# A residual-add and RMSNorm kernel: every bulk transfer cut into two halves of 64 partitions

## Chip, cores and metric

The kernel runs on one core of one Trainium2 chip. The metric is the device time of one execution in microseconds (us); lower is better. The record marks each run as fast or slow, by its clock and its time against its fellows. Repeated runs of the kernel before agree within 0.03%.

## The reference

```python
# x, residual: (32, 2048, 2048) float32; gamma: 2048 ones; eps 1e-6
z = x + residual
rms = np.sqrt(np.mean(z ** 2, axis=-1, keepdims=True) + eps)
return (z / rms * gamma).astype(np.float32)
```

65536 rows of 8 KB: two inputs are read, one output is written, 1610.6 MB in all.

## The kernel before

Rows lie on the 128 partitions of SBUF, the on-chip memory, R = 7 consecutive rows on each partition. The first two tiles have 3 and 5 rows per partition, the other 72 have 7. For each tile one transfer loads x into one of two buffers `z`, one loads the residual into a shared area; VectorE adds in place, ScalarE squares and sums, VectorE scales in place, and one transfer stores `z`. One queue (SP) issues all of it. A transfer raises its semaphore by U = 16 (the trace has 3712 landings for 232 transfers, 16 each).

```python
    def rows(t, i):
        k = sizes[i]
        return t[starts[i] : starts[i] + P * k, :].rearrange("(p r) m -> p r m", r=k)
    # ... (cut)
    def load_x(sp, t, d=0):
        i = t.i + d
        inc(sp.dma_start(out=z[i % 2][:, : sizes[i], :], in_=rows(x_f, i)), "x_in", i)
    # ... load_r likewise (cut)
    def sp_turn(sp, t):
        i = t.i
        t.wait(sp, "done", -1)         # tile i-1 is scaled
        inc(sp.dma_start(out=rows(o_f, i - 1), in_=z[(i - 1) % 2][:, : sizes[i - 1], :]), "s_out", i - 1)
        if i == last:
            return
        t.wait(sp, "add_a")            # first part of tile i is added
        load_r(sp, t, 1)
        t.wait(sp, "s_out", -1)        # tile i-1 is stored, its z is free
        # ... the last tile's x comes in four pieces (cut)
        load_x(sp, t, 1)
```

Of the kernel before, what the change touches and what calls it, by code (L numbers as in the profile page):

```python
# [9 lines left out]
def kernel(  # L10
# [18 lines left out]
    P = nc.NUM_PARTITIONS  # L29
# [4 lines left out]
    x_f = x.flatten_outer_dims()  # L34
    r_f = residual.flatten_outer_dims()
    o_f = out.flatten_outer_dims()
# [1 line left out]
    n_rows, D = x_f.shape  # L38
    R = 7
    STEP = 4  # L40
    U = 16
    lead = [3, 5]
    n_full = (n_rows // P - sum(lead)) // R
    sizes = lead + [R] * n_full
# [5 lines left out]
    last = n_tiles - 1  # L50
# [6 lines left out]
# [3 lines that stand above are left out]
# [3 lines left out]
    def sb(name, shape):  # L63
        return ctx.enter_context(nc.sbuf_tensor(name, shape, fp32))
# [6 lines left out]
    def sem(name):  # L71
        sems.append(ctx.enter_context(nc.semaphore(name)))
        return sems[-1]
# [3 lines left out]
    z = [sb(f"z{p}", [P, R, D]) for p in range(2)]  # L77
    r_area = sb("r_area", [P, R + STEP, D])
# [12 lines left out]
    ev = {k: [sem(f"{k}{p}") for p in range(2)] for k in names}  # L91
    x_tail = [sem(f"x_tail{k}") for k in range(4)]
    g_in = sem("g_in")
    dve = sem("dve_own")
    act = sem("act_own")
    s_tail = sem("s_tail")
# [6 lines left out]
    def entry(i):  # L103
        if i == 0:
            return R + STEP - sizes[0]
        return 0 if i % 2 else STEP
# [7 lines left out]
    class Turn:  # L114
# [5 lines left out]
        def at(self, d):  # L120

            n = ((self.i + d) // 2 + 1) * U
            return n if self.it is None else self.it * (U // 2) + n

# [3 lines left out]
    def inc(ins, kind, i):  # L128
        return ins.then_inc(ev[kind][i % 2], U)


    def load_x(sp, t, d=0):
        i = t.i + d
        inc(sp.dma_start(out=z[i % 2][:, : sizes[i], :], in_=rows(x_f, i)), "x_in", i)

    def load_r(sp, t, d=0):
        i = t.i + d
        e = entry(i)
        inc(
            sp.dma_start(out=r_area[:, e : e + sizes[i], :], in_=rows(r_f, i)),  # L140
            "r_in",
            i,
        )

    def sp_turn(sp, t):
        i = t.i
        t.wait(sp, "done", -1)
        inc(
            sp.dma_start(out=rows(o_f, i - 1), in_=z[(i - 1) % 2][:, : sizes[i - 1], :]),
            "s_out",  # L150
            i - 1,
        )
        if i == last:
            return
        t.wait(sp, "add_a")
        load_r(sp, t, 1)
        t.wait(sp, "s_out", -1)
        if i + 1 == last:
            for k, (a, b) in enumerate(tail):
                sp.dma_start(  # L160
                    out=z[last % 2][:, a:b, :], in_=rows(x_f, last)[:, a:b, :]
                ).then_inc(x_tail[k], U)
        else:
            load_x(sp, t, 1)


    def add(v, i, a, b):
        e = entry(i)
        s = z[i % 2][:, a:b, :]
        return v.tensor_add(out=s, in0=s, in1=r_area[:, e + a : e + b, :])  # L170

    def scale(v, i, a, b, rs, c=0):
        for g in range(a, b):
            s = z[i % 2][:, g, :]
            ins = v.scalar_tensor_tensor(  # L175
                out=s,
                in0=s,
                scalar=rs[:, c + g - a : c + g - a + 1],
                in1=gamma_tile[:, :],
                op0=mult,  # L180
                op1=mult,
            )
        return ins

    def dve_turn(v, t, own):
        i, p = t.i, t.p
        t.wait(v, "x_in")
        t.wait(v, "r_in")
        (a0, b0), (a1, b1) = parts(i)
        inc(add(v, i, a0, b0), "add_a", i)  # L190
        inc(add(v, i, a1, b1), "add_b", i)
        for h, (a, b) in enumerate(parts(i)):
            n = b - a
            t.wait(v, "rms_a" if h == 0 else "rms_b")
            v.reciprocal(out=rstd[p][h][:, :n], in_=rms[p][h][:, :n]).then_inc(dve, U)  # L195
            v.wait_ge(dve, own(i, h))
            ins = scale(v, i, a, b, rstd[p][h])
        inc(ins, "done", i)
# [50 lines left out]
    def sync_program(sp):  # L249
        load_x(sp, Turn(0))  # L250
        load_r(sp, Turn(0))

        sp.wait_ge(tail_ev["add"], 1)
        for q in range(4):
            sp.dma_start(  # L255
                out=stage[32 * q : 32 * q + 1],
                in_=gamma.partition_broadcast(1).rearrange("p (a b) -> p a b", a=16),
            ).then_inc(g_in, U)
        load_r(sp, Turn(1))
        load_x(sp, Turn(1))  # L260
        for i in range(1, n_tiles):
            sp_turn(sp, Turn(i))
        for k, (a, b) in enumerate(tail):
            sp.wait_ge(tail_ev["done"], k + 1)
            sp.dma_start(
                out=rows(o_f, last)[:, a:b, :], in_=z[last % 2][:, a:b, :]
            ).then_inc(s_tail, U)
        sp.wait_ge(s_tail, U * len(tail))
        sp.wait_ge(ev["s_out"][(last - 1) % 2], ((last - 1) // 2 + 1) * U)
        sp.sem_inc(fin, 1)  # L270

    def vector_program(v):
        v.memset(eps_tile[:, :], float(eps))  # L273
        v.memset(stage, 0.0).then_inc(tail_ev["add"], 1)  # L274
        v.wait_ge(g_in, 4 * U)
        v.stream_shuffle(gamma_tile[:, :].rearrange("p (a b) -> p a b", a=16), stage, [0] * 32)  # L276
        for i in range(LO):
            dve_turn(v, Turn(i), lambda i, h: (2 * i + h + 1) * U)
        with v.Fori(0, 2 * n_iter, 2) as it:
            for i in range(LO, LO + 2):  # L280
                dve_turn(v, Turn(i, it), lambda i, h: it * (2 * U) + (2 * i + h + 1) * U)
        for i in range(HI, last):
            dve_turn(v, Turn(i), lambda i, h: (2 * i + h + 1) * U)
        base = 2 * last * U
        t = Turn(last)
        t.wait(v, "r_in")

        def tail_scale(k):
            a, b = tail[k]
            v.wait_ge(tail_ev["rms"], k + 1)  # L290
            v.reciprocal(out=tail_rstd[:, a:b], in_=tail_rms[:, a:b]).then_inc(dve, U)  # L291
            v.wait_ge(dve, base + (k + 1) * U)
            scale(v, last, a, b, tail_rstd, a).then_inc(tail_ev["done"], 1)

        for k, (a, b) in enumerate(tail):
            v.wait_ge(x_tail[k], U)
            add(v, last, a, b).then_inc(tail_ev["add"], 1)
            if k:
                tail_scale(k - 1)
        tail_scale(len(tail) - 1)  # L300

    def scalar_program(s):
# [13 lines left out]
        for k, (a, b) in enumerate(tail):  # L316
# [4 lines left out]
            ).then_inc(tail_ev["rms"], 1)  # L321

    sync_program(nc.sync)
    vector_program(nc.vector)
    scalar_program(nc.scalar)

# [40 lines left out]
```

## Time and profile before

| | kernel before |
|---|---|
| time, median | 3726.5 us |
| transfers: busy share, rate | 99.9%, 434 GB/s in the steady part |
| VectorE / ScalarE busy | 62% / 29% |
| bulk transfers | 228 |
| tile period | 50.8 us |
| packet of 57344 B (one partition of a full tile) | 2.116 us |

The page, the stretch from 1000 to 2000 us, the queue's issues and two links of the chain are shown and read in the prediction: the transfer engines run without a gap (99.9%) at a fixed pace (99.7% of the packets of 57344 B took below 2.22 us), and all else hides behind them. The packet row needs a remark. Besides the page, the trace records each packet's size, start and duration, and each transfer's landings, but no engine number. I take a landing, and the small packet that goes with it (3712 of each in the kernel before), as one for each engine that took part.

### The profile page before, as it was taken

How to read it: one execution, taken by the hardware profiler on the slowest of the kernel's cores; microseconds unless marked ns; L12 is line 12 of the kernel's file. 1: busy time of each engine (PE TensorE's matmuls, PEld its weight loads, DVE VectorE, ACT ScalarE, POOL GpSimd, SP SyncE). 2: the span in 40 equal slices, each digit the busy share in tenths (PEclk: the TensorE clock that was granted, in tenths of full speed). 3: DMA queues.
4: the chain of work that ended last, by engine and by line, in shares of the span. 5: the costliest groups of instructions: out<-in, count | busy, mean ns of one | idle time of the engine just before them, and what ended most of it. 6: DMA issues, size and time to landing. Idle time of an engine off the chain costs nothing.

```text
span 3724.7 us, 3652 instructions
## 1 busy us (share of the span) xinstructions
DVE 2302.5 (62%) x816; ACT 1072.4 (29%) x1176; POOL 0.2 (0%) x4
## 2 busy tenths in 40 slices
DVE  5666665566665566665566665566665566655566
ACT  2233322233322233322233322233322233322233
POOL 0000000000000000000000000000000000000000
DMA  9999999999999999999999999999999999999999
GB/s 420 432 434 434 434 434 434 432 434 434 435 434 434 434 434 436 434 434 434 433 434 434 434 434 434 434 434 434 434 434 434 434 434 434 434 434 434 434 434 398
DMA packets 32964, 1610.69 MB, mean 432 GB/s; under 512 B 3712, under 2 KB 3776, under 8 KB 3776
## 3 DMA queue, kind: packets, MB, share of 16 engines
q1 hardware_dynamic: 32960, 1610.66, 99.9%
q14 instruction: 4, 0.03, 0.0%
HBM read 1073.77 MB, written 536.87 MB: 432 GB/s over the span
## 4 chain that ended last, share of the span: by engine, by line
DMA 66%; DVE 22%; issue 9%; ACT 2%; SPq 0%; DVEq 0%; ACTq 0%
DMA out_dram<-z 33%; DMA z<-in_x_dram 33%; DVE z L170 15%; DVE z L175 7%; ACT sq_junk L221 1%; DMA r_area<-in_gamma_dram 0%; ACT rms L229 0%; DVE rstd L195 0%; DVEq L126 0%; SPq L255 0%; DVE r_area L274 0%; ACTq L209 0%; ACTq L126 0%; DVE tail_rstd L291 0%; SPq L160 0%
## 5 line engine op out<-in xcount | busy, mean ns | idle before, releaser
L170 DVE TENSOR_TENSOR z<-z,r_area 128x8192 f32<-128x8192 f32 (+2 forms) x150 | 1109.4, 7437 | 1253.2 <-DMA z<-in_x_dram 1227.6
L221 ACT ACTIVATE sq_junk<-z 128x2048 f32<-128x2048 f32 x512 | 963.4, 1882 | 2618.1 <-DVE z L170 2606.7
L175 DVE SCALAR_TENSOR_TENSOR z<-z,rstd,gamma_tile 128x2048 f32<-128x2048 f32 x505 | 1153.5, 2344 | 5.2
L195 DVE RECIPROCAL rstd<-rms 128x4 f32<-128x4 f32 (+2 forms) x146 | 25.3, 173 | 130.8 <-ACT rms L229 130.8
L221 ACT ACTIVATION_READ_ACCUMULATOR sq_junk<-z 128x1 f32 x512 | 95.4, 186 | 0.0
L229 ACT ACTIVATE rms<-ssq,eps_tile 128x4 f32<-128x4 f32 (+2 forms) x146 | 43.3, 297 | 13.4
L175 DVE SCALAR_TENSOR_TENSOR z<-z,tail_rstd,gamma_tile 128x2048 f32<-128x2048 f32 x7 | 16.2, 2346 | 0.1
L276 DVE LOAD_MASK_SELECT gamma_tile<-r_area x1 | 0.0, 14 | 16.4 <-DMA r_area<-in_gamma_dram 16.4
L276 DVE STREAM_SHUFFLE gamma_tile<-r_area 128x2048 f32<-128x2048 f32 x1 | 2.3, 2290 | 0.0
L274 DVE MEMSET r_area<- 128x2048 f32 x1 | 1.8, 1765 | 0.4 <-issue 0.4
L221 ACT ACT_TABLE_LOAD x1 | 1.3, 1283 | 0.9 <-SPq L75 0.9
L229 ACT ACT_TABLE_LOAD x1 | 1.3, 1283 | 0.1
L229 ACT ACTIVATE tail_rms<-tail_ssq,eps_tile 128x2 f32<-128x2 f32 (+1 forms) x4 | 1.2, 296 | 0.1
L273 DVE MEMSET eps_tile<- 128x1 f32 x1 | 0.1, 59 | 1.0 <-SPq L75 1.0
L291 DVE RECIPROCAL tail_rstd<-tail_rms 128x2 f32<-128x2 f32 (+1 forms) x4 | 0.6, 158 | 0.0
L348 POOL MEMSET const-bfloat16-1.0<- 128x1 bf16 x1 | 0.1, 102 | 0.0
L348 POOL MEMSET const-uint8-127<- 128x1 uint8 x1 | 0.1, 102 | 0.0
L348 POOL MEMSET const-float32-1.0<- 128x1 f32 x1 | 0.1, 99 | 0.0
L348 POOL MEMSET const-float32-0.0<- 128x1 f32 x1 | 0.1, 98 | 0.2 <-issue 0.2
## 6 DMA issues: line engine op xcount, KB each, us to landing
r_area<-in_residual_dram SPq DMA_DIRECT2D x72, 7168.0 KB, 27.2
z<-in_x_dram SPq DMA_DIRECT2D x71, 7168.0 KB, 33.8
out_dram<-z SPq DMA_DIRECT2D x71, 7168.0 KB, 34.5
z<-in_x_dram SPq DMA_DIRECT2D x3, 2048.0 KB, 26.3
out_dram<-z SPq DMA_DIRECT2D x3, 2048.0 KB, 13.9
r_area<-in_residual_dram SPq DMA_DIRECT2D x1, 5120.0 KB, 25.3
z<-in_x_dram SPq DMA_DIRECT2D x1, 5120.0 KB, 36.8
out_dram<-z SPq DMA_DIRECT2D x1, 5120.0 KB, 24.7
```

What stands on the lines that cost most here:

```text
L170: return v.tensor_add(out=s, in0=s, in1=r_area[:, e + a : e + b, :])
L175: ins = v.scalar_tensor_tensor(out=s, in0=s, scalar=rs[:, c + g - a : c + g - a + 1], in1=gamma_tile[:, :], op0=mult, op1=mult,)
L195: v.reciprocal(out=rstd[p][h][:, :n], in_=rms[p][h][:, :n]).then_inc(dve, U)
L221: s.activation(out=sq_junk[:, :], in_=src[:, g, :], func=Act.Square, accum_out=sq[:, g - a : g - a + 1],)
L229: return s.activation(out=rm, in_=sq[:, : b - a], func=Act.Sqrt, bias=eps_tile[:, :], scale=inv_d)
L273: v.memset(eps_tile[:, :], float(eps))
L274: v.memset(stage, 0.0).then_inc(tail_ev["add"], 1)
L276: v.stream_shuffle(gamma_tile[:, :].rearrange("p (a b) -> p a b", a=16), stage, [0] * 32)
L291: v.reciprocal(out=tail_rstd[:, a:b], in_=tail_rms[:, a:b]).then_inc(dve, U)
L348: nc = _bacc.Bacc("TRN2", target_bir_lowering=False, num_devices=1)
```

## The change

The intent: each of the 16 transfer engines should have 4 packets in each of two transfers, instead of 8 in one (a transfer before has 128 packets of data, one for each partition, and 16 landings). The core of the diff (the call sites are cut; all bulk loads and stores go through `move`):

```diff
-    U = 16
+    U = 32
+    def move(sp, out, in_, s):
+        for h in range(2):
+            c = slice(h * P // 2, (h + 1) * P // 2)
+            sp.dma_start(out=out[c], in_=in_[c]).then_inc(s, 16)
@@ load_x, and so on
-        inc(sp.dma_start(out=z[i % 2][:, : sizes[i], :], in_=rows(x_f, i)), "x_in", i)
+        move(sp, z[i % 2][:, : sizes[i], :], rows(x_f, i), ev["x_in"][i % 2])
```

Below, A is the lower half (partitions 0 to 63) and B the upper (64 to 127).

More of the change, by code (lines that the diff above doesn't have):

```diff
@@ L138, in load_r @@
         e = entry(i)
-        inc(
-            sp.dma_start(out=r_area[:, e : e + sizes[i], :], in_=rows(r_f, i)),
-            "r_in",
-            i,
-        )
+        move(sp, r_area[:, e : e + sizes[i], :], rows(r_f, i), ev["r_in"][i % 2])
     def sp_turn(sp, t):
@@ L147, in sp_turn @@
         t.wait(sp, "done", -1)
-        inc(
-            sp.dma_start(out=rows(o_f, i - 1), in_=z[(i - 1) % 2][:, : sizes[i - 1], :]),
-            "s_out",
-            i - 1,
-        )
+        move(sp, rows(o_f, i - 1), z[(i - 1) % 2][:, : sizes[i - 1], :], ev["s_out"][(i - 1) % 2])
         if i == last:
@@ L159, in sp_turn @@
             for k, (a, b) in enumerate(tail):
-                sp.dma_start(
-                    out=z[last % 2][:, a:b, :], in_=rows(x_f, last)[:, a:b, :]
-                ).then_inc(x_tail[k], U)
+                move(sp, z[last % 2][:, a:b, :], rows(x_f, last)[:, a:b, :], x_tail[k])
         else:
@@ L257, in sync_program @@
                 in_=gamma.partition_broadcast(1).rearrange("p (a b) -> p a b", a=16),
-            ).then_inc(g_in, U)
+            ).then_inc(g_in, 16)
         load_r(sp, Turn(1))
@@ L264, in sync_program @@
             sp.wait_ge(tail_ev["done"], k + 1)
-            sp.dma_start(
-                out=rows(o_f, last)[:, a:b, :], in_=z[last % 2][:, a:b, :]
-            ).then_inc(s_tail, U)
+            move(sp, rows(o_f, last)[:, a:b, :], z[last % 2][:, a:b, :], s_tail)
         sp.wait_ge(s_tail, U * len(tail))
@@ L274, in vector_program @@
         v.memset(stage, 0.0).then_inc(tail_ev["add"], 1)
-        v.wait_ge(g_in, 4 * U)
+        v.wait_ge(g_in, 4 * 16)
         v.stream_shuffle(gamma_tile[:, :].rearrange("p (a b) -> p a b", a=16), stage, [0] * 32)
```

## The prediction

The forecast's sum came to 7271 + 10 us: 7271 is 3709.6 us at the full rate times 1.96. No trace of the kernel before shows that factor, 2 less 0.04 for a lead of 0.3 us between engines. The 217 GB/s is half of the 434 measured. "In step" means that all 16 engines are on the same half at a time.

> **What bounds the kernel now.** I read the page's overview first: which engine is busy, and how busy the transfers are.
>
> ```profile
> DVE 2302.5 (62%) x816; ACT 1072.4 (29%) x1176; POOL 0.2 (0%) x4
> DMA  9999999999999999999999999999999999999999
> DMA packets 32964, 1610.69 MB, mean 432 GB/s; under 512 B 3712, under 2 KB 3776, under 8 KB 3776
> q1 hardware_dynamic: 32960, 1610.66, 99.9%
> HBM read 1073.77 MB, written 536.87 MB: 432 GB/s over the span
> ```
>
> No compute engine is above 62%, the transfer engines are at nine tenths or more in all forty slices, and their packets fill 99.9% of the span of 16 engines. Next I asked for a long stretch far from both ends.
>
> ```profile
> 1000.00:2000.00 1000.00, 624.21 (x220) 292.27 (x320) 0.00 (x0) 1.00 1.00 434
> ```
>
> The columns are the stretch, its length, the busy time of DVE, ACT and POOL, the clock, the transfer share (1.00) and GB/s (434). So the kernel streams at one rate: 1610.69 MB at 434.2 GB/s (16 engines at 27.1) take 3709.6 us, and only 15 of the 3724.7 us are left for start and end. The trace also has each packet's duration: a packet of 57344 bytes (7 rows of 2048 float32, one partition of a full tile) takes 2.116 us at the median, 27.1 GB/s for its engine, with almost no scatter. The engines run at a fixed pace.
>
> Then the issuing queue, in time order near the end of the steady part, and two links of the chain of waits there:
>
> ```profile
> 3594.36 0.33 SPq L140 DMA_DIRECT2D r_area<-in_residual_dram  x1
> 3604.67 0.33 SPq L134 DMA_DIRECT2D z<-in_x_dram  x1
> 3620.98 0.34 SPq L149 DMA_DIRECT2D out_dram<-z  x1
> 3645.16 0.33 SPq L140 DMA_DIRECT2D r_area<-in_residual_dram  x1
> ...
> 3553.85 33.84 DMA z<-in_x_dram
> 3620.98 34.47 DMA out_dram<-z
> ```
>
> One tile period is 3645.16 - 3594.36 = 50.8 us, three transfers of 7.34 MB at 434 GB/s (16.9 us each). The x load lands 33.84 us after its issue: 16.9 behind the residual load already queued, 16.9 of its own. The store takes 34.47 for the same reason. The tightest point is the residual load, issued 10.3 us (3604.67 - 3594.36) before the engines have finished the store in front of it. The queue never runs dry, so neither waits nor issue cost count; only the rate does.
>
> [...] no transfer here covers 64, so the half rate is not shown. [...] 228 bulk transfers and 4 of gamma, times 16 completions, are the 3712 packets under 512 B. [...]
>
> **The change part by part.**
> *Bytes and data packets*: unchanged. 74 residual loads, 77 x loads (four are the pieces of the last tile) and 77 stores become 456 transfers of 64 partitions, with one packet for each partition as before; 228 x 16 = 3648 completion packets are added, of 9 ns each in this trace: 2 us per engine, little.
> *Issue*: 228 more issues of 0.34 us, 78 us of a queue that otherwise waits (1689.2 us for the add, 1190.8 for the scale). Per tile 1.0 us, and each second half is queued long before the first is through: beside the work.
> *Waits*: the unit of every transfer semaphore rises from 16 to 32, so each wait is still for a whole tile; VectorE's and ScalarE's order and shapes are the same. Nothing to pay or gain.
> [...]
> *Relief from drift*: [...] From the trace's landing records (16 for each transfer) I took the spread between the first and the last engine: about 1.1 us in the first 200 us, 3.3 at 900, 6.6 at the end, where one engine trails. [...]
> *Ends*: at half rate the last x pieces and the last stores are always queued behind transfers, so idle time there shrinks; I leave 10 us for start and the last landing.
> Sum: 7271 + 10[...]: I say 7270.
>
> **The rivals.**
> 1. *Engines slip out of step*: [...] Then the full 434 GB/s return: 3727 to 3760 us. [...] I give 0.11.
> 2. *Only loads are limited*: [...] Then 1073.77 MB at 217 (4946 us) and 536.87 at 434 (1236): 6182 us. [...] About 0.1.
> 3. *Partial overlap*: [...] Some 0.15 together.
> 4. *A gain*: an earlier half lets nothing start earlier, as all waits are for both halves[...]. Only the 15 us at the ends could shrink: 0.4%. Faster by 2% would need a rate of 443: 0.01.
>
> **Range and chances.** In step (7100 to 7450) I hold at 0.63; with rivals 2 and 3 the range from 6150 to 7480 holds a little over 8 in 10. Slower by over 2%: 0.88; within 2%: 0.11; faster: 0.01.
>
> **What would show it.** In the profile of the changed kernel: (a) slices at 217 to 222 GB/s instead of 434, with the transfer share still at nine tenths or above, because the packets take longer, not because the queue is dry. (b) Packets of 57344 bytes near 4.2 us instead of 2.116; 2.1 for those of stores would be rival 2; 2.1 for all is rival 1. (c) A tile period near 101 us (6 x 16.9) instead of 50.8. (d) VectorE's and ScalarE's busy times as before; VectorE's share falls to 31 or 32%, its wait for x grows from 1227.6 to about 4900 us. (e) Residual loads landing about 44 (A) and 61 us (B) after issue instead of 27.2: the 10.3 of the store's remainder become 27, plus 16.9 for each half. (f) 7360 small packets, (456 + 4) x 16; fewer would mean that a half does not run on 16 engines and that my engine picture is wrong. The prediction fails if the rate stays near 434 with (f) as said[...].

## The result, and the profile after

The changed kernel takes 7100.4 us (median of 4, 7042.9 to 7108.3), 1.9025 times the time before (95% interval 1.8938 to 1.9112). Ratios here are the mean time of one kernel's fast runs over that of the other's of the same rounds, so not quite the ratio of the medians quoted. The prediction of 7270 us (6150 to 7480) was 2.4% above. The profiled execution is the fastest one, of 7041.1 us.

The page of the changed kernel, the lines that answer to those shown of before:

```profile
DVE 2302.6 (33%) x816; ACT 1072.4 (15%) x1176; POOL 0.2 (0%) x4
DMA  9999999999999999999999999999999999999999
DMA packets 36614, 1610.72 MB, mean 229 GB/s; under 512 B 7360, under 2 KB 7424, under 8 KB 7424
q1 hardware_dynamic: 36608, 1610.67, 99.7%
```

The busy times and the bytes are the same, the engines are as busy as before (99.7%, 99.9% then), and the rate is about half (229 GB/s, 432 then). The busy share cannot tell the two kernels apart; the rate and the packets' durations can (4.005 us at the mean for one of 57344 B, 2.118 before).

The same stretch as before, the queue's issues, and one link of the chain of the changed kernel, each from its own view (the columns are those of the same views of before):

```profile
1000.00:2000.00 1000.00, 314.12 (x110) 146.12 (x160) 0.00 (x0) 1.00 1.00 227
```
```profile
3076.79 3.21 SPq L135 DMA_DIRECT2D r_area<-in_residual_dram  x2
3098.16 1.28 SPq L135 DMA_DIRECT2D z<-in_x_dram  x2
3103.41 1.13 SPq L135 DMA_DIRECT2D out_dram<-z  x2
3173.74 3.22 SPq L135 DMA_DIRECT2D r_area<-in_residual_dram  x2
```
```profile
3103.39 63.69 another core or an unknown queue
```

The tile period is 3173.74 - 3076.79 = 97.0 us instead of 50.8. The store is now issued 5.3 us after the x load, before even the residual load is through, which lands 56.6 us after its first issue at the median (before the change the store came 16.3 us after the x load): VectorE is done long before, and the transfers alone set the pace. The chain's "another core or an unknown queue" is the wait for x. Why the chain does not name it is not known (in `e1_rows` below two transfers raise one semaphore as well, and there it is named). The waits of the compute engines do name it, and how long it was:

```profile
DVE z L165 <- DMA z<-in_x_dram: 4537.5, 74, 65.6
```

VectorE waits 4537.5 us for x in all, 1227.6 before.

Of the packets of 57344 B, from the trace's packet records:

| kernel | mean us | median us | below 2.22 us | 2.22 to 4 us | above 4 us |
|---|---|---|---|---|---|
| before | 2.118 | 2.116 | 99.7% | 0.3% | 0 |
| after | 4.005 | 4.384 | 7% | 18% | 75% |

The mean accounts for the time: 3709.6 x 4.005 / 2.118 = 7015 us, of the 7041 in this execution.

### The profile page after: what moved, and what is told of

Read it like the earlier page. It is cut to its first block, busy times and chain, and to the rows that moved or that the text cites. A ratio compares the mean times of both kernels' runs of the same rounds, so it can differ in the third digit from the quotient of the medians.

```text
span 7041.1 us, 3880 instructions
## 1 busy us (share of the span) xinstructions
DVE 2302.6 (33%) x816; ACT 1072.4 (15%) x1176; POOL 0.2 (0%) x4
## 2 busy tenths in 40 slices
DMA packets 36614, 1610.72 MB, mean 229 GB/s; under 512 B 7360, under 2 KB 7424, under 8 KB 7424
## 3 DMA queue, kind: packets, MB, share of 16 engines
q1 hardware_dynamic: 36608, 1610.67, 99.7%
## 4 chain that ended last, share of the span: by engine, by line
another core or an unknown queue 64%; DVE 23%; issue 9%; ACT 2%; DMA 1%; DVEq 0%; SPq 0%; ACTq 0%
DVE z L165 16%; DVE z L170 7%; ACT sq_junk L216 1%; DMA z<-in_x_dram 1%; DMA r_area<-in_gamma_dram 0%; ACT rms L224 0%; DVE rstd L190 0%; SPq L135 0%; DVEq L126 0%; DVEq L272 0%; SPq L250 0%; ACTq L204 0%; ACTq L126 0%; DVE tail_rstd L284 0%
## 5 line engine op out<-in xcount | busy, mean ns | idle before, releaser
L165 DVE TENSOR_TENSOR z<-z,r_area 128x8192 f32<-128x8192 f32 (+2 forms) x150 | 1109.4, 7437 | 4537.5 <-DMA z<-in_x_dram 4537.5
```

The costliest lines, as they stand in the source:

```text
L165: return v.tensor_add(out=s, in0=s, in1=r_area[:, e + a : e + b, :])
```

## The experiments

Twelve kernels ran, for five questions. All give the right result except two that say so. Kernels that were run together ran on one chip, and the kernel before ran beside each of them.

**Is it the number of transfers?** `e1_rows` has as many transfers, issues and completions as the change, but cuts each by rows.

```diff
-            c = slice(h * P // 2, (h + 1) * P // 2)
-            sp.dma_start(out=out[c], in_=in_[c]).then_inc(s, 16)
+            # cut = (k + 1) // 2 of the k rows; a single row is cut by columns
+            c = (slice(None), slice(0, cut) if h == 0 else slice(cut, k))
+            sp.dma_start(out=out[c], in_=in_[c]).then_inc(s, 16)
```

> Every bulk transfer in two as in the change, but cut by rows: 456 transfers of all 128 partitions. [...] packets run at 27.1 GB/s as in the kernel before, and the time is 3727 us, at most 3740. Rival, that 456 transfers instead of 228, their issues, completions or waits for two cost the time: about 7100 us as in the changed kernel, or at least well above 4000.

Measured: 3741.5 us, ratio 1.0041 (1.0024 to 1.0058). The number of transfers costs 15 us, not 3374. The packets alone account for that: those of 4 and 3 rows took 1.2146 and 0.9141 us at the mean, together 10.5 ns more than one of 7 rows, which is 18 us over the 1712 that each engine moves. The page of this run has as many small packets (7360, the completions) as that of the changed kernel:

```profile
DMA packets 65798, 1610.72 MB, mean 431 GB/s; under 512 B 7360, under 2 KB 7424, under 8 KB 7936
```

**Loads or stores?** `e2_loads` halves the loads by partitions and cuts the stores by rows; `e3_stores` is the mirror.

```diff
# e2_loads: the stores
-        move(sp, rows(o_f, i - 1), z[(i - 1) % 2][:, : sizes[i - 1], :], ...)
+        rows_move(sp, rows(o_f, i - 1), z[(i - 1) % 2][:, : sizes[i - 1], :], ...)
# e3_stores: the loads
-        move(sp, z[i % 2][:, : sizes[i], :], rows(x_f, i), ...)
+        rows_move(sp, z[i % 2][:, : sizes[i], :], rows(x_f, i), ...)
```

The sums of 5940 and 4820 us below are for both directions slowed, each by a factor of 1.9.

> Loads in halves of 64 partitions as in the change, stores cut by rows (128 partitions). [...] the loads are two thirds of the bytes, so 3710 x (2/3 x 1.9 + 1/3) = about 5940 us; packets of loads near 4.4 us, of stores 2.1. Only loads limited (rival): about as slow as the whole change, 7000 to 7100 us. Only stores limited: 3727 us. [...] the loads' factor may lie anywhere from 1.7 to 2.1: 5600 to 6300.

> The mirror: stores in halves of 64 partitions, loads cut by rows. [...] 3710 x (2/3 + 1/3 x 1.9) = about 4820 us (4600 to 5100). Only loads limited (rival): 3727 us. The excesses over 3727 of this run and of the one with halved loads should add to about the 3374 us of the whole change.

Measured: 6424.4 us (ratio 1.7235, 1.7206 to 1.7264) and 4574.8 us (1.2295, 1.2266 to 1.2325). Both directions are slowed, so the rival "only loads" falls. Against the row-cut kernel's 3741.5 the halved loads cost 2683 us and the halved stores 833; together 3516, and the whole change costs 3359 on that base: they nearly add. The loads took 2.08 times their share (2683 over their 2473 us, plus 1), the stores 1.67 times (833 over 1236, plus 1; a part of it lies beside the stores: their packets alone give 3.357 / 2.118 = 1.59, and the row-cut loads between them are slower too, 1.2585 and 0.9253 us for 4 and 3 rows). My 5940 and 4820 used one factor for both, and missed: loads are slowed more, stores less. The packets of 57344 B show it (in these two runs they are the halved ones alone):

| kernel | mean us | below 2.22 us | 2.22 to 4 us | above 4 us |
|---|---|---|---|---|
| e2_loads | 4.389 | 0.2% | 3% | 97% |
| e3_stores | 3.357 | 29% | 30% | 42% |

**Is it 64 partitions, or which 64?** `e4_lower` moves the lower half only, `e9_middle` the middle partitions 32 to 95 only; both give a wrong result and have the same shapes, bytes and transfers. `e8_evenodd` gives the right result with even and odd partitions as its two halves, and `e10_quarters` goes from two consecutive groups to four.

```diff
# e4_lower (one transfer, U = 16; the other partitions are set to zero at the start)
+        c = slice(0, P // 2)
# e9_middle (likewise)
+        c = slice(P // 4, 3 * P // 4)
# e8_evenodd
-            c = slice(h * P // 2, (h + 1) * P // 2)
+            c = slice(h, P, 2)
# e10_quarters (U = 64)
+        for h in range(4):
+            c = slice(h * P // 4, (h + 1) * P // 4)
```

The expectations for `e9_middle` and `e10_quarters` each give two times: the first is the author's own, the second that of a rival.

> Wrong result on purpose: only the lower half (partitions 0 to 63) of every transfer is moved, half of the bytes (805 MB), the upper half of the tiles is set to zero once. [...] the time stays near that of the kernel before although the bytes are halved: 3720 us [...] (packets of 57344 B at 4.23 us), 3930 us if each pays what most packets of the changed kernel show (4.45 us). If the slowdown comes from the number of transfers [...]: near 2300 to 2600 us, where the vector engine would limit. [...]

> Wrong result on purpose, as the run that moved only the lower half, but it moves the middle partitions 32 to 95. [...] 27.1 GB/s each, and the time falls to where the vector engine limits, about 2350 to 2450 us. [...] the middle is as slow as the lower half: 3584 us, packets mostly near 4.45 us.

> Two transfers of 64 partitions again, but the even and the odd partitions instead of the lower and the upper half. [...] If the span of one transfer decides [...]: 3727 to 3800 us. [...] Slow because a transfer has 64 partitions at all: 7100 us.

> The change taken one step further: four transfers of 32 consecutive partitions[...]. [...] about 7100 us. [...] packets near 8.5 to 9 us and 13500 to 14800 us in all.

Measured:

| kernel | time us | ratio to before (95% interval) | mean packet us | above 4 us |
|---|---|---|---|---|
| e4_lower | 3584.1 | 0.9612 (0.9596 to 0.9628) | 3.964 | 71% |
| e9_middle | 2543.1 | 0.6825 (0.6813 to 0.6836) | 2.191 | 0 |
| e8_evenodd | 3730.3 | 1.0010 (0.9994 to 1.0027) | 2.119 | 0 |
| e10_quarters | 7103.5 | 1.9071 (1.9039 to 1.9103) | 4.036 | 77% |

The pages of `e4_lower` and of `e9_middle`, VectorE's busy time, the bytes and the share of the queue:

```profile
DVE 2343.8 (65%) x821; ACT 1072.4 (30%) x1176; POOL 0.2 (0%) x4
...
DMA packets 18372, 805.39 MB, mean 225 GB/s; under 512 B 3712, under 2 KB 3776, under 8 KB 3776
...
q1 hardware_dynamic: 18368, 805.35, 97.4%
```
```profile
DVE 2378.4 (94%) x826; ACT 1072.4 (42%) x1176; POOL 0.2 (0%) x4
...
DMA packets 18372, 805.39 MB, mean 317 GB/s; under 512 B 3712, under 2 KB 3776, under 8 KB 3776
...
q1 hardware_dynamic: 18368, 805.35, 75.8%
```

The same 18372 packets and 805 MB. On the lower half the engines are busy for 97.4% at 225 GB/s, and half of the bytes take nearly the time of all of them; on the middle they idle a quarter of the time at 317 GB/s, and VectorE (94%) has become the bound. Only the partitions differ (and with them which rows of DRAM are moved, in the same shape), so it is neither the count of 64, nor the shape, nor the transfers' size, but which partitions they are (3.964 us for a packet at the mean on the lower half, 2.191 on the middle). Quarters of 32 consecutive partitions take the same time as halves of 64 (7103.5 and 7100.4 us). The rival's times (3584 us for the middle, 13500 to 14800 for the quarters) fell in both runs. Why these sets of partitions differ no run shows. Two sums missed. `e9_middle` is 93 us above my 2350 to 2450; the zeroing alone cost VectorE 75.8 us (2378.4 against 2302.6), and the first store left at 126.6 us, against 39.5 before. `e4_lower` is below my 3720 and 3930: 9% of its packets took under 2.22 us, and its 225 GB/s are more than the 217, half of 434, of the prediction. By the matching in point 4 below, the fast ones are packets of stores. The even and the odd partitions, the two-way split closest to the change, cost nothing:

```profile
DMA packets 36614, 1610.72 MB, mean 432 GB/s; under 512 B 7360, under 2 KB 7424, under 8 KB 7424
```

This line of `e8_evenodd` has the packets of the changed kernel, to the last one, at 432 GB/s.

**Are the engines slow because they run in step?** The changed kernel with one extra copy from DRAM to DRAM, queued once on some of the engines ahead of tile 2's residual load, in order to put them out of step with the others. Eight engines took it in `e5` and `e6` and four in `e7`, by the small packets (7368, 7368 and 7364, 7360 in the changed kernel); in `e11` one engine was late, by the landings below. Under test is an estimate of mine, that with a lead d a half takes 2 - d/8.45 of its old time (8.45 us is half of a transfer's 16.9). The copy fills rows of the output that are overwritten at the end, after a wait for the copy.

```diff
+        if i == 1:   # e5: 8 rows of 28 * 8 KB; e6: 8 of 14 * 8 KB; e7: 4 of 28 * 8 KB
+            c = [q[b : b + 8 * 40, :].rearrange("(p r) m -> p r m", r=40)[:, :28, :] for q in (o_f, x_f)]
+            # e11: 29 rows of 8 KB, so that one engine does it
+            c = [q[b : b + 58, :].rearrange("(r t) m -> r t m", t=2)[:, 0, :] for q in (o_f, x_f)]
+            sp.dma_start(out=c[0], in_=c[1]).then_inc(ahead, 16)
         load_r(sp, t, 1)
```

> The changed kernel with one extra copy, DRAM to DRAM, of 8 rows of 229376 B, queued once ahead of the residual load of tile 2: [...] it should keep only 8 of the 16 engines busy (8.5 us if an engine copies DRAM to DRAM at 27 GB/s, 17 us if at half of that). The halves are unchanged. Theory [...]: if [...] the delay is near 8.5 us, [...] the time returns to near 434 GB/s, 3730 to 4300 us. If the delay is 17 us (a whole transfer), they are in step again, though one transfer apart, and the time stays within a few per cent of 7100. Rival, that a transfer of 64 partitions is slow in itself [...]: 7100 whatever the delay.

> The same with half the bytes (114688 B for each of 8 engines): 4.2 us or 8.5 us of delay. Out of step by 4.2 of 8.45 us: factor 2 - 0.5 = 1.5, so 5500 to 5800 us if the lead keeps; by 8.5 us: 3730 to 4300 us. Together with the run of 229376 B one of the two should be clearly below 6000 us under the in-step theory; under the rival both stay at 7100.

> The same copy of 229376 B on 4 engines only. [...] the next transfers wait for all 16 engines: I expect 6600 to 7100 us, little gain, though the longer copy of 8 engines gains. [...]

> The changed kernel with the one extra DRAM to DRAM copy shaped so that one single engine does it (29 rows of 8192 B, about 8.8 us at 27 GB/s), ahead of the residual load of tile 2. With 8 or 4 engines delayed no packet of the next loads was fast[...]. [...] the time stays near 7100 us (7000 to 7200)[...]. If no packet gets fast, being in step is not what makes the packets slow.

Measured: 7093.4, 7110.1, 7113.3 and 7091.6 us; ratios 1.9064 (1.9004 to 1.9124), 1.9081 (1.9047 to 1.9116), 1.9096 (1.9064 to 1.9128) and 1.9016 (1.8955 to 1.9077). All are as slow as the changed kernel. The delay itself took hold. By the landing records, A of the next residual load landed with 8 engines 7.3 to 8.0 us behind the first one and the other 8 within 2.0 us in `e5`; with 4 engines 11.2 to 11.7 us behind and 12 within 5.4 in `e7`; with one engine 11.5 us behind and the others within 6.3 in `e11`. Yet from 114.5 to 160 us no packet was fast: the fastest took 4.34, 4.24, 4.25 and 4.13 us in `e5`, `e6`, `e7` and `e11`, and 4.12 in the changed kernel. Nor was there relief while the copy ran: of the packets of 57344 B that started between 107 and 112 us in `e5`, those of the copy took 2.12 us, and those of the eight engines on A 4.48 to 4.51, though the other eight were on the copy, DRAM to DRAM; in `e11`, with one engine away, 4.15 to 4.50. In `e11` the late engine landed A 5.2 us after the last of the others, which had landed theirs by then, and its packets were as slow as theirs (none below 4.13 us). So in these runs an engine did not get its full pace back when it, or another, was late by several us. My picture of the drift, in which a lead d shortens each half to 2 - d/8.45, falls.

**Is an engine slow on a half when only eight work?** `e12_eight` cuts each transfer in sixteen of 8 partitions four apart, each within one half. Eight engines work (50.0% of the time of 16, below).

```diff
-    U = 32
+    U = 256   # VectorE's own semaphore keeps steps of 16
-        for h in range(2):
-            c = slice(h * P // 2, (h + 1) * P // 2)
+        for h in range(16):
+            b = 32 * (h // 4) + h % 4
+            c = slice(b, b + 29, 4)
```

> Every bulk transfer in sixteen of 8 partitions, four apart (0, 4, ... 28, then 1, 5, ... 29, and so on), [...] each transfer stays within one half. This tells what makes an engine slow in the halves, after the delayed engines stayed slow. (i) [...] all packets near 2.12 us, and 8 engines at 27.1 GB/s take 2 x 3710 = 7420 us. (ii) [...] packets of one half 2.1, of the other 4.2 to 4.5, 11000 to 11700 us. (iii) Any transfer within one half is slow in itself, whatever the other engines do: all packets 4.2 to 4.5, 14800 to 15700 us. I hold (i) and (iii) as about equally likely.

Measured: 7507.2 us, ratio 2.0141 (2.0108 to 2.0175). The page of this run, the shares of the transfers in 40 slices, their rates, the packets and the queue:

```profile
DMA  4555555555555555554555545545545455554554
GB/s 211 216 217 216 216 217 216 217 216 217 216 216 217 216 217 216 216 217 216 217 216 214 215 213 215 215 213 215 215 213 214 214 215 215 215 215 213 215 215 185
DMA packets 58527, 1611.02 MB, mean 215 GB/s; under 512 B 29248, under 2 KB 29312, under 8 KB 29312
...
q1 hardware_dynamic: 58496, 1610.76, 50.0%
```

The share of 16 engines is 50.0%: eight work all the time, as the small packets say too ((3648 x 8) + 64 = 29248). Packets of 57344 B take 2.127 us at the mean, 98.6% of them below 2.22, on both halves. So a transfer within one half is not slow in itself, and an engine was at full pace on either half: (i) came out, (ii) and (iii) fall. Set beside the changed kernel: eight engines at full pace move 215 GB/s, sixteen on the same halves 229. The second eight add about 6%. But this run changes more than the number of engines at work: an engine has one packet in each transfer instead of four, and the partitions lie four apart. Which of these restores the pace was not tested, and in `e5` eight engines on A, with the others away, stayed slow (4.48 to 4.51 us).

## Why the prediction was right, point by point

The time was right because which partitions a transfer covers decided its pace here (4.005 us for a packet at the mean with consecutive halves, 2.119 with even and odd partitions). Why it does was not shown. The account of engines in step was wrong, and that two errors of size nearly cancelled was luck.

1. *The bound before, the bytes, the issues and the waits.* Right. The busy times are unchanged, the 7360 small packets are there, and `e1_rows` prices the 228 extra transfers at 0.4%. Two sums were off without weight: 16 engines at 27.1 GB/s are 433.6, not 434.2; and the issues took 316 us more in all (395.5 against 79.1), not 78, but stayed beside the work (in `e8_evenodd` they take 273.3 us, at no cost in time).
2. *Consecutive halves at half rate.* Right, and near in size: 227 GB/s in the long stretch where I said 217 to 222. No transfer of the kernel before covers 64 partitions, so the half rate was not shown beforehand. Shown by the runs: which partitions are moved decides (3.964 us for a packet at the mean in `e4_lower` against 2.191 in `e9_middle`, 4.005 in the change against 2.119 in `e8_evenodd`), both directions are slowed (4.389 in `e2_loads`, 3.357 in `e3_stores`), and the eight engines of `e12_eight` lose nothing in pace (2.127). What makes a half slow is not shown.
3. *The price of a half.* Mis-sized. I took 4.23 us for a packet, twice 2.116, as an estimate. The halved loads alone took 4.389 (209 GB/s for 16 engines), so lying in one half cost a load 2.07 times, and the halved loads cost 2683 us more, where twice the pace would have cost 2473.
4. *The relief.* Mis-sized, and for a wrong reason. I took a factor of 1.96 from a lead of 0.3 us, an estimate, for loads and stores alike. The mean packet gives 1.89, and nearly all of the relief is in the stores: in the runs that halve one direction alone, 29% of the stores' packets are fast, 0.2% of the loads'. In `e4_lower`, where consecutive packets of an engine can be matched best by their ends and starts, those of loads run at 4.4 to 4.5 us, and the four of the store behind them at about 2.3, 2.1, 3.5 and 4.5. Points 3 and 4 err in opposite directions, and so the sum came within 2.4%: that closeness is luck.
5. *In step.* Wrong. The step that the engines keep the distances they start with fell in the changed kernel itself: the 32 landings of a residual load (A and B) should span little over one half, 17.5 us (4 packets of 4.384), if the engines were in step. They span 23.0 us at 119 us, 38.7 at 292, and 38.0 at the median from there on. So the first and the last engine drift about 20 us apart, over a whole half, and the packets stay slow (75% above 4 us); nor did the four delayed kernels gain. What makes the engines slow stays open. The run with eight engines (2.127 us for a packet) points to the number at work; against it, eight engines on A in `e5` took 4.48 to 4.51 us while the other eight were away, and the sixteen of `e8_evenodd` 2.119. Which partitions of a transfer go to which engine no run shows. Also open is what lets the first packets of a store run fast.
6. *The rivals.* Slipping out of step to the full rate did not happen; "only loads" is refuted; the partial overlap exists in size (229 GB/s, where half of 434 is 217), in the stores (3.357 us for a packet, 4.389 for one of a load). There was no gain.
7. *The marks.* The period was 97.0 us for my 101, the packets 4.384 at the median for 4.2, VectorE's share 33% for 31 or 32, its wait for x 4537.5 for about 4900: the period, the share and the wait follow from the stores' relief, which I had too small, the packets' median from the price of a half (point 3). The last landing of a residual load came 56.6 us after its first issue at the median, for my 61; A's own landings can't be told from B's.

No version with the right result beat the kernel before: the row-cut and the even-odd kernel come within 0.4% and 0.1% of it, as its engines already run at their fixed pace (2.116 us for a packet).

## What to carry to other kernels

Where transfers set the pace, look at the rate and the packets' durations, not at the busy share: 99.9% at 434 GB/s and 99.7% at 229 look the same there. If a transfer must be cut, try the rows or alternate partitions first, whose pieces still span both halves of SBUF: those kernels took 3741.5 and 3730.3 us here, for 3726.5 uncut. Pieces within one half, of 64 or of 32 consecutive partitions, ran at about half the rate (7100.4 and 7103.5 us; a packet of the halved loads took 2.07 times as long as before, one of the halved stores 1.59 times), and queuing the other half behind did not give that back.
